# A seven-product feed-forward: two plain first tiles, no additions on POOL, two weight sums by an accumulating DMA, sums read from PSUM

## The chip, the cores and the metric

The kernel runs on one core of one Trainium2 chip. A core has five engines that run their own queues in order and wait for each other by semaphores: PE (TensorE) multiplies matrices, DVE (VectorE) and ACT (ScalarE) do arithmetic on 128 partitions and reach both SBUF and PSUM, POOL (GpSimd) does arithmetic in SBUF and issues DMAs of its own kind, SP (SyncE) issues the other DMAs. Matrix products land in PSUM, in 8 banks of 128 x 512 floats. The metric is the device time of the whole program in microseconds (us); lower is better.

## What is computed

One inference step of a small two-layer backbone of width 1024 over 640 tokens: 512 latent tokens and 128 context tokens, which are held side by side as columns 0 to 511 and 514 to 641 of a feature-major tile of 642 columns (512 and 513 are a gap of zeros). Every sub-layer is an RMSNorm, a shift and scale that come from the conditioning vector, the sub-layer itself, and a gated addition to the residual stream. The part of the reference that the change touches is the feed-forward of the second layer and the output projection ahead of it:

```python
def conv_ffn(h, w_up, conv_w, conv_b, w_down):
    a, b = jnp.split(h @ w_up, 2, axis=-1)
    a = dwconv(a, conv_w, conv_b)
    return (jax.nn.silu(a) * b) @ w_down
...
        x = x + g1 * (mix @ p['w_out'][i])
        h = rmsnorm(x, p['norm_ffn'][i]) * (1.0 + sc2) + sh2
        x = x + g2 * conv_ffn(h, p['ffn_w_up'][i], p['ffn_conv_w'][i], p['ffn_conv_b'][i], p['ffn_w_down'][i])
```

`w_up` has 2 x 2816 columns: 22 tiles of 128 columns for `a` and 22 for `b`.

## The kernel before

**Precision.** Every operand of the large products is split into a rounded part and a rest (`h` and `l`). ACT writes the rounded part (a cast), DVE subtracts it from the source for the rest, and `mm3` (lines 302 to 306) issues three matmuls for one product: high by high, high by low, low by high.

**Seven products.** In the second layer the feed-forward takes a tile `f` of `a` and the tile `f` of `b` together. The two weight tiles are a 2 x 2 block matrix (rows: the first and the last 512 features; columns: `a` and `b`), and the tokens are cut in two blocks of 320. Both factors are thus 2 x 2 blocks, and Winograd's form of Strassen's scheme makes the four blocks of the result from seven block products in place of eight, at the price of sums of blocks of both factors. `Blocks` holds the token blocks a11, a12, a21, a22 and the sums s1 to s4; `norm_blocks` fills them; `block_weights` makes the weights' sums (four additions of 128 x 512 on DVE per tile) and splits the seven weight operands; `up_unit` issues the seven products (12 matmuls of 320 columns each) into PSUM banks X, Y and V, keeps four of them in SBUF by ACT copies (`keep`: q1, u2, q5, u3), and adds: `ar` and one part of `br` on DVE, the other part of `br` on POOL from two SBUF copies (line 603). `give` then does the convolution, the SiLU and the gate, and splits the result into `g`; the rest `g.l` is a POOL subtraction (line 633).

**Order of the work.** `project_out` multiplies by an output weight matrix, 8 output tiles `d`, in two halves of the columns: `HALVES` 0 to 383 and 384 to 641. With a follower (`then`) the first four tiles run whole, and the last four run first half by first half and then second half by second half. After the first of the second halves, `norm_stats` makes the first half's norm factors (squares summed over partitions by matmuls with a column of ones, the power on POOL, a broadcast by matmuls, an ACT copy to `rb`); after the second of them `then(0, rb)` is called, which for this layer is `norm_blocks` of half 0. After the last tile come `norm_stats` and `norm_blocks` of half 1. The token blocks are cut at column 320 and the halves at 384, so half 0 fills a11 and a12 whole and 64 columns each of a21 and a22; half 1 fills their rest, and makes and splits the sums.

`ffn_blocks` runs 22 tiles in groups of 8, 7 and 7 (`FGROUPS`), each group followed by a `project_out` of the down projection. Only a11 and a12 exist early, so in the first group the first two products of tiles 0 and 1 are issued ahead (`next(u)`) before either tile goes on.

**What sets the order on an engine.** The framework queues each engine's instructions at build time: an instruction earlier in the program goes first, but one that is expected to have its inputs sooner may be put ahead of it. A tile with `bufs=n` waits for the release of the buffer n tiles back. The raw weights (`wr`) have 3 buffers. The split weights have 4 rooms (2 pools of 2); `split_w` takes a room, `split_op` half a room. While the last four tiles of `project_out` are open they hold all four rooms.

**Layer 0** has the same `project_out` with the same follower scheme, but a plain feed-forward (`ffn`): its follower `into` splits the first two weight pairs into `pre`, and `ffn` multiplies four first halves before it needs any second half.

Of the kernel before, what the change touches and what calls it, by code (L numbers as in the profile page):

```python
# [81 lines left out]
def hybrid_kernel(ctx: ExitStack, tc: tile.TileContext, A, O):  # L82
# [280 lines left out]
    def norm_stats(acc, rb, hf, last=None):  # L363

        cs = HCHUNKS[hf]
        n = len(cs)
        ps = s_ps("ss")  # L370
        for i, t in enumerate(cs):
            c = slice(COFF[t], COFF[t] + 128)
            nc.tensor.matmul(ps[:, i : i + 1], acc[:, c], ones, start=True, stop=last is None)
# [3 lines left out]
        nc.vector.tensor_scalar(out=v, in0=ps[:, :n], scalar1=1.0 / D, scalar2=EPS, op0=ALU.mult, op1=ALU.add)
        rs = tmp.tile([P, 3], F32, tag="nr", name=nm("nr"))[:, :n]
        rsqrt(rs, v, n)
        ps = s_ps("rb")  # L380
        for i in range(n):
            nc.tensor.matmul(ps[:, BLK[i]], rs[:, i : i + 1].broadcast_to([P, P]), ident, start=True, stop=True)
        if last is not None:
            return ps
        if hf == 0:
            nc.scalar.copy(rb[:, :384], ps[:, :384])
        else:
            nc.gpsimd.memset(rb[:, 512:514], 0.0)
            nc.scalar.copy(rb[:, 384:512], ps[:, :128])
            nc.scalar.copy(rb[:, PO:NT], ps[:, 128:256])  # L390
# [82 lines left out]
    class Blocks:  # L473
# [18 lines left out]
        def split(self, n, k, src, eng=None):  # L492
            if n not in self.hi:
                self.hi[n], self.lo[n] = (slot(n + t_, (P, 4, ST), F32R) for t_ in "hl")
            h_ = self.hi[n][:, k, :]
            nc.scalar.copy(h_, src)
# [5 lines left out]
    def norm_blocks(x, rb, layer, w, B, hf):  # L502

        c0, c1 = HALVES[hf]

        def norm(d):
            k, f = d % 4, d // 4
            t = tmp.tile([P, NT], F32, tag="ft" if d % 2 else "fs", name=nm("nt"))
            nc.vector.tensor_tensor(out=t[:, c0:c1], in0=x[d // 2][:, d % 2, c0:c1], in1=rb[:, c0:c1], op=ALU.mult)
            for i, parts in enumerate(SPARTS):  # L510
                to = B.raw((("a11", "a12"), ("a21", "a22"))[i][f], k)
                for a, b, o in parts:
                    a_, b_ = max(a, c0), min(b, c1)
                    if a_ < b_:
                        m = 0 if a < PO else 1
                        nc.scalar.activation(
                            to[:, o + a_ - a : o + b_ - a], t[:, a_:b_], AF.Identity,
                            scale=scl[:, layer, w, d, m : m + 1], bias=mcol(layer, 0 if w == 0 else 3, d, m),
                        )

        if hf == 0:
            for d in range(KD):
                norm(d)
                n = ("a11", "a12")[d // 4]
                B.split(n, d % 4, B.raw(n, d % 4), nc.vector if d % 2 == 0 else nc.gpsimd)
            return
        for k in range(4):
            norm(k)
            norm(k + 4)
            a11, a12, a21, a22 = (B.raw(n, k) for n in ("a11", "a12", "a21", "a22"))  # L530
            s1 = tmp.tile([P, NT], F32, tag="fs", name=nm("s1"))[:, :ST]
            nc.vector.tensor_tensor(out=s1, in0=a22, in1=a21, op=ALU.subtract)
            nc.vector.tensor_tensor(out=a11, in0=a11, in1=a21, op=ALU.subtract)
            nc.vector.scalar_tensor_tensor(out=a21, in0=a11, scalar=-1.0, in1=a22, op0=ALU.mult, op1=ALU.subtract)
            nc.vector.scalar_tensor_tensor(out=a12, in0=a21, scalar=-1.0, in1=a12, op0=ALU.mult, op1=ALU.subtract)
            for n, src in (("s2", a21), ("s1", s1), ("s3", a11), ("s4", a12), ("a22", a22)):
                B.split(n, k, src)
# [1631 lines left out]
```

## Time and profile before

| | us |
|---|---|
| median of 3 runs (1921.46 to 1929.83) | 1925.57 |
| the profiled execution | 1924.54 |
| its span, first to last instruction | 1922.7 |
| what lies around the span | 1.84 |
| PE busy (share of the span) | 1821.7 (95%) |
| DVE busy | 1311.0 (68%) |
| ACT busy | 791.1 (41%) |
| POOL busy | 424.0 (22%) |
| mean granted TensorE clock | 0.983 |

Busy time of PE is not PE at its peak, since a matmul's record overlaps the next one's. So the text below reads PE by the starts of its matmuls. A group of instructions is shown as: line, engine, operation, output<-inputs, shapes, count, then busy time and mean of one, then the idle time ahead of them and who ended it. A stage of the windows view shows for each engine the busy time and, in brackets, how many instructions it had, then the granted clock, the DMA share and GB/s.

### The profile page before, as it was taken

The numbers are of one execution on the slowest core, as the hardware profiler recorded it, in microseconds if no ns is written. First come the engines' busy times: TensorE is split into PE (matmuls) and PEld (weight loads), VectorE is DVE, ScalarE is ACT, GpSimd is POOL, SyncE is SP. The second block draws the span as 40 slices with busy tenths as digits, with TensorE's granted clock in tenths as the row PEclk, the third lists the DMA queues.
The fourth block names the chain that finished last, engine by engine and source line by source line (L and its number), as shares of the span: only waits on it lengthen the run. The fifth ranks groups of instructions, "written<-read, shape, count | busy, mean of one in ns | idle before, by whom it ended". The sixth has DMA issues, their size and how long they took to land. (4 is left out here: it accounts for less than half of the span.)

```text
span 1922.7 us, 31316 instructions
## 1 busy us (share of the span) xinstructions
PE 1821.7 (95%) x12248; PEld 1694.0 (88%) x12248; DVE 1311.0 (68%) x2624; ACT 791.1 (41%) x1544; POOL 424.0 (22%) x445
## 2 busy tenths in 40 slices
PE   5899999999889999999999999999997999999998
PEld 1578999998667999999999998978796999999998
DVE  4755666667797669757677647655648974875974
ACT  3555443343232263313312324544537651652653
POOL 2323442325554011101100103410001220220221
PEclk9899999999999999999999999999997999999999
DMA  8332112225453335434343222201211231222221
GB/s 287 123 102 75 44 46 73 71 65 188 155 189 105 143 144 187 133 129 143 115 160 127 75 90 99 92 23 50 78 45 44 88 100 55 78 83 72 88 88 56
DMA packets 66189, 197.46 MB, mean 103 GB/s; under 512 B 6872, under 2 KB 18520, under 8 KB 65914
## 3 DMA queue, kind: packets, MB, share of 16 engines
q1 hardware_dynamic: 52000, 176.71, 27.3%
q10 hardware_dynamic: 14042, 18.76, 2.8%
q8 instruction: 96, 1.57, 0.3%
q14 instruction: 51, 0.42, 0.1%
HBM read 178.91 MB, written 16.54 MB: 102 GB/s over the span
## 5 line engine op out<-in xcount | busy, mean ns | idle before, releaser
L298 ACT CAST wwh<-wr 128x1024 fp32r<-128x1024 f32 (+1 forms) x136 | 139.1, 1023 | 302.9 <-PE mm L305 277.4
L305 PE MATMUL mm<-h1l,wwh 128*128 128x384 f32 (+2 forms) x704 | 219.0, 311 | 0.9 <-DVE h1l L406 0.9
L306 PE MATMUL mm<-h1h,wwl 128*128 128x384 f32 (+2 forms) x704 | 218.9, 311 | 0.0
L304 PE MATMUL mm<-h1h,wwh 128*128 128x384 f32 (+2 forms) x704 | 218.5, 311 | 0.0
L299 DVE TENSOR_TENSOR wwl<-wr,wwh 128x1024 fp32r<-128x1024 f32 (+1 forms) x136 | 167.6, 1233 | 60.3 <-ACT wwh L298 60.1
L422 DVE SCALAR_TENSOR_TENSOR x<-mm,mod,x 128x128 f32<-128x128 f32 (+1 forms) x192 | 78.2, 436 | 168.6 <-PE mm L306 168.5
L250 DVE SCALAR_TENSOR_TENSOR mjunk<-mraw,crow 128x512 f32<-128x512 f32 x192 | 150.3, 795 | 2.7 <-ACT crow L238 1.5
L304 PE MATMUL mm<-h0h,wwh 128*128 128x384 f32 (+2 forms) x448 | 148.9, 332 | 0.5 <-DVE d L823 0.2
L305 PE MATMUL mm<-h0l,wwh 128*128 128x384 f32 (+2 forms) x448 | 140.3, 313 | 0.0
L306 PE MATMUL mm<-h0h,wwl 128*128 128x384 f32 (+2 forms) x448 | 139.4, 311 | 0.0
L699 DVE SCALAR_TENSOR_TENSOR cv<-mm,par,cv 128x382 f32<-128x382 f32 (+3 forms) x184 | 100.2, 546 | 57.2 <-ACT cv L693 56.1
L305 PEld LDWEIGHTS mm<-h1l,wwh 128*128 128x128 f32 x704 | 133.1, 189 | 1.8 <-DVE h1l L406 1.6
L306 PEld LDWEIGHTS mm<-h1h,wwl 128*128 128x128 f32 x704 | 132.9, 189 | 0.0
L304 PEld LDWEIGHTS mm<-h1h,wwh 128*128 128x128 f32 x704 | 132.6, 188 | 0.2 <-ACT h1h L405 0.2
L550 ACT CAST cwh<-wr 128x512 fp32r<-128x512 f32 x132 | 79.5, 622 | 79.8 <-PE mm L305 23.2
L551 DVE TENSOR_TENSOR cwl<-wr,cwh 128x512 fp32r<-128x512 f32 x132 | 99.4, 772 | 12.5 <-ACT cwh L550 12.4
L304 PE MATMUL od<-owh,h2h 128*128 128x256 f32 x320 | 98.4, 308 | 0.4 <-ACT h2h L405 0.4
L1112 POOL TENSOR_TENSOR am<-a,msk 128x512 fp32r<-128x512 f32 x60 | 73.0, 1225 | 91.9 <-PE Q L1141 81.3
L306 PE MATMUL od<-owh,h2l 128*128 128x256 f32 x320 | 90.5, 286 | 1.9 <-DVE h2l L406 1.1
L305 PE MATMUL od<-owl,h2h 128*128 128x256 f32 x320 | 90.7, 284 | 0.0
L693 ACT ACTIVATE cv<-mm,par 128x383 f32<-128x383 f32 x92 | 50.6, 550 | 94.5 <-PE mm L306 89.7
L304 PEld LDWEIGHTS mm<-h0h,wwh 128*128 128x128 f32 x448 | 85.4, 191 | 3.1 <-issue 1.8
(540 smaller groups left out, 5479.5 us busy)
## 6 DMA issues: line engine op xcount, KB each, us to landing
wr<-in_w_up SPq DMA_DIRECT2D x88, 512.0 KB, 3.2
wr<-in_w_mod SPq DMA_DIRECT2D x48, 512.0 KB, 4.5
mraw<-in_w_modT SPq DMA_DIRECT2D x48, 512.0 KB, 3.5
wr<-in_w_in SPq DMA_DIRECT2D x28, 512.0 KB, 3.3
wr<-in_w_dn SPq DMA_DIRECT2D x32, 448.0 KB, 3.3
wr<-in_w_out SPq DMA_DIRECT2D x16, 512.0 KB, 3.2
wr<-in_w_dn SPq DMA_DIRECT2D x16, 512.0 KB, 3.6
wr<-in_od_w_in SPq DMA_DIRECT2D x16, 512.0 KB, 4.0
```

What stands on the lines that cost most here:

```text
L250: nc.vector.scalar_tensor_tensor(out=junk, in0=raw[:, c], scalar=1.0, in1=rows[m][:, c], op0=ALU.mult, op1=ALU.mult, accum_out=part[:, d, ...
L298: nc.scalar.copy(hi[:, :K], src)
L299: nc.vector.tensor_tensor(out=lo[:, :K], in0=src, in1=hi[:, :K].bitcast(F32), op=ALU.subtract)
L304: nc.tensor.matmul(ps, l[0](k), r[0](k), start=start, stop=False, skip_group_check=more)
L305: nc.tensor.matmul(ps, l[0](k), r[1](k), start=False, stop=False, skip_group_check=more)
L306: nc.tensor.matmul(ps, l[1](k), r[0](k), start=False, stop=stop, skip_group_check=more)
L422: nc.vector.scalar_tensor_tensor(out=xt[:, a:b], in0=ps[:, a - c0 : b - c0], scalar=mcol(layer, ch, d, m), in1=xt[:, a:b], op0=ALU.mult, o ...
L550: nc.scalar.copy(hi, src)
L551: nc.vector.tensor_tensor(out=lo, in0=src, in1=hi.bitcast(F32), op=ALU.subtract)
L693: nc.scalar.activation(t[:, o0:o1], p[:, o0 - a : o1 - a], AF.Identity, scale=w[1], bias=0.0 if bias is None else bias)
L699: nc.vector.scalar_tensor_tensor(out=t[:, c0:c1], in0=p[:, c0 + s_ - a : c1 + s_ - a], scalar=w[i], in1=t[:, c0:c1], op0=ALU.mult, op1=ALU ...
L1112: eng.tensor_tensor(out=v(out), in0=v(a32), in1=msk[:, lv, :, None, :].broadcast_to([P, 2, 2, P]), op=ALU.mult)
```

## The change

- `project_out` of layer 1, `norm_stats` and `residual` take the cut of the halves as an argument. The new cut `SCUT` is 0 to 319 and 320 to 641, the cut of the token blocks, so that half 0 fills a11 and a12 and half 1 fills a21 and a22. The norm factors of a half are made for chunks of 128 or 64 tokens, with one DVE and one POOL operation per run of chunks of equal height (for `SCUT` two of each, one before). With `SCUT` the last square isn't added into `acc`, and half 1 reads its factors from PSUM, without the ACT copies.
- `then(0, rb)` is called after the last tile's second half (`soon=3`), not after the second tile's.
- The follower `to_blocks` splits the weights of tiles 0 and 1 (`up_w`) into `pre`.
- Tiles 0 and 1 of the feed-forward are plain (`plain_unit`): 8 products a tile, first both tiles' columns 0 to 319, then the rest.
- The sums of the token blocks are made behind the first halves, by `combine`, for two feature blocks at a time (128 x 640), half of them ahead of tile 0's second half and half ahead of tile 1's.
- `block_weights`: two plain loads of 256 KB put w11 and w12 into a new tile `t13`, and a DMA that POOL issues adds the whole `b` tile (w12 and w22 side by side) onto it, so that `t13` holds t1 and t3. Two additions on DVE remain. `t13` has 2 buffers.
- `up_unit`: the part of `br` that POOL added is added on DVE, straight from PSUM bank X; the copy `u3` goes. All seven products of a tile are issued in one go.
- `give`: `g.l` and, in `norm_blocks`, every rest is made on DVE, none on POOL. The scratch for POOL's DMAs grows from 1024 to 2048.

```diff
+CUT = (HALVES, HPARTS, (((0, 128), (128, 256), (256, 384)), ((384, 512), (PO, NT))))
+SCUT = (
+    ((0, 320), (320, NT)), (((0, 320, 0),), ((320, 512, 0), (PO, NT, 1))),
+    (((0, 128), (128, 256), (256, 320)), ((320, 384), (384, 512), (PO, NT))),
+)
...
-                if hf == 1 and d == first + 1:
+                if hf == 1 and d == first + soon:
                     then(0, rb)
...
     def norm_blocks(x, rb, layer, w, B, hf):
...
+        c0, c1 = SCUT[0][hf]
+        for k in range(4):
+            for f in range(2):
+                d, n = k + 4 * f, ("a11", "a12", "a21", "a22")[2 * hf + f]
+                t = tmp.tile([P, NT], F32, tag="ft" if f else "fs", name=nm("nt"))
+                r_ = rb[:, c0:c1] if hf == 0 else rb[:, : c1 - c0]
+                nc.vector.tensor_tensor(out=t[:, c0:c1], in0=x[d // 2][:, d % 2, c0:c1], in1=r_, op=ALU.mult)
+                to = B.raw(n, k)
+                for a, b, o in SPARTS[hf]:
+                    m = 0 if a < PO else 1
+                    s_, b_ = scl[:, layer, w, d, m : m + 1], mcol(layer, 0 if w == 0 else 3, d, m)
+                    if m:
+                        nc.vector.tensor_scalar(
+                            out=to[:, o : o + b - a], in0=t[:, a:b], scalar1=s_, scalar2=b_, op0=ALU.mult, op1=ALU.add
+                        )
+                    else:
+                        nc.scalar.activation(to[:, o : o + b - a], t[:, a:b], AF.Identity, scale=s_, bias=b_)
+                B.split(n, k, to)
+
+    def combine(B, k):
+
+        kk = slice(k, k + 2)
+        a11, a12, a21, a22 = (B.raws[n][:, kk, :] for n in ("a11", "a12", "a21", "a22"))
+        s1 = tmp.tile([P, NT], F32, tag="fs", name=nm("s1"))[:, : 2 * ST].rearrange("p (k t) -> p k t", k=2)
+        nc.vector.tensor_tensor(out=a11, in0=a11, in1=a21, op=ALU.subtract)
+        nc.vector.tensor_tensor(out=s1, in0=a22, in1=a21, op=ALU.subtract)
+        nc.vector.scalar_tensor_tensor(out=a21, in0=a11, scalar=-1.0, in1=a22, op0=ALU.mult, op1=ALU.subtract)
+        B.split("s2", kk, a21)
+        B.split("s1", kk, s1)
+        B.split("s3", kk, a11)
+        nc.vector.scalar_tensor_tensor(out=a12, in0=a21, scalar=-1.0, in1=a12, op0=ALU.mult, op1=ALU.subtract)
+        B.split("s4", kk, a12)
...
-    def block_weights(a, b, pool):
+    def block_weights(layer, f, pool):
...
+        t13 = pool.tile([P, 1024], F32, tag="t13", name=nm("t13"), bufs=2)
+        nc.sync.dma_start(t13[:, :512], w_a[:, :512])
+        nc.sync.dma_start(t13[:, 512:], w_b[:, :512])
+        nc.gpsimd.dma_start(t13, w_b, accum_op=ALU.add)
+        t1, t3 = (t13[:, 512 * i : 512 * i + 512].rearrange("p (k c) -> p k c", k=4) for i in range(2))
+        a = load_raw(w_a, KD)
+        w11, w21 = a[:, :4], a[:, 4:]
+        w22 = load_raw(w_b[:, 512:], 4)
         yield split_op(w11)
         yield split_op(w21)
...
+        TT(out=w11, in0=t1, in1=w22, op=ALU.add)
         yield split_op(w11)
+        yield split_op(t1)
+        yield split_op(t3)
         yield split_op(w22)
-        TT(out=w21, in0=w21, in1=t2, op=ALU.add)
+        TT(out=w21, in0=w21, in1=w11, op=ALU.add)
         yield split_op(w21)
...
+    def plain_unit(wa, wb, f, B, outs, give):
+
+        ar, br = (outs[f % 2][:, i, :] for i in range(2))
+        for hf in range(2):
+            ps = []
+            for w in (wa, wb):
+                ps.append(mm_ps("pu"))
+                for k in range(KD):
+                    n = ("a11", "a12", "a21", "a22")[2 * hf + k // 4]
+                    l, r = wl_of(w), B.of(n)
+                    mm3(ps[-1][:, :ST], l, ((lambda k: r[0](k % 4)), (lambda k: r[1](k % 4))), k, k == 0, k == KD - 1)
+            for a, b, o in SPARTS[hf]:
+                nc.scalar.copy(ar[:, a:b], ps[0][:, o : o + b - a])
+                nc.vector.tensor_copy(br[:, a:b], ps[1][:, o : o + b - a])
+            if hf == 0:
+                yield
+        give(f, ar, br, 1.0)
...
-        u3 = keep("u3", X)
         for a, b, o in SPARTS[1]:
-            nc.gpsimd.tensor_tensor(out=br[:, a:b], in0=u3[:, o : o + b - a], in1=q5[:, o : o + b - a], op=ALU.add)
+            nc.vector.tensor_tensor(out=br[:, a:b], in0=X[:, o : o + b - a], in1=q5[:, o : o + b - a], op=ALU.add)
...
-                nc.gpsimd.tensor_tensor(out=g.l(k, 0, NT), in0=s, in1=g.h(k, 0, NT).bitcast(F32), op=ALU.subtract)
+                nc.vector.tensor_tensor(out=g.l(k, 0, NT), in0=s, in1=g.h(k, 0, NT).bitcast(F32), op=ALU.subtract)
...
+                us = [plain_unit(*pre[2 * f : 2 * f + 2], f, B, outs, give) for f in range(2)]
+                for u in us:
+                    next(u)
+                for k, u in zip((0, 2), us):
+                    combine(B, k)
+                    next(u, None)
+                f1 = 2
+            for f in range(f1, f0 + n):
+                up_unit(layer, f, B, pool, outs, give)
...
+    def to_blocks(hf, rb):
+        if hf == 0:
+            norm_blocks(x, rb, 1, 1, hb, hf)
+            pre.extend((up_w(1, 0), up_w(1, NF)))
+        else:
+            pre.extend((up_w(1, 1), up_w(1, NF + 1)))
+            norm_blocks(x, rb, 1, 1, hb, hf)
+
+    project_out(x, mix, 1, 2, wout(1), KD, to_blocks, cut=SCUT, soon=3)
```

More of the change, by code (lines that the diff above doesn't have):

```diff
@@ L385, in norm_stats @@
         if hf == 0:
-            nc.scalar.copy(rb[:, :384], ps[:, :384])
+            c1 = cut[0][0][1]
+            nc.scalar.copy(rb[:, :c1], ps[:, :c1])
         else:
             nc.gpsimd.memset(rb[:, 512:514], 0.0)
-            nc.scalar.copy(rb[:, 384:512], ps[:, :128])
-            nc.scalar.copy(rb[:, PO:NT], ps[:, 128:256])
+            for a, b, _ in cut[1][1]:
+                nc.scalar.copy(rb[:, a:b], ps[:, a - c0 : b - c0])
     def norm_mod(x, rb, layer, w, act, hf, ds=range(KD)):
@@ L416, in sq_acc, with residual @@
             nc.vector.tensor_tensor(out=acc[:, c0:c1], in0=acc[:, c0:c1], in1=q[:, c0:c1], op=ALU.add)
-    def residual(x, d, ps, layer, ch, hf):
+    def residual(x, d, ps, layer, ch, hf, cut=CUT):
         xt = x[d // 2][:, d % 2, :]
-        c0 = HALVES[hf][0]
-        for a, b, m in HPARTS[hf]:
+        c0 = cut[0][hf][0]
+        for a, b, m in cut[1][hf]:
             nc.vector.scalar_tensor_tensor(
@@ L431, in load_x, with project_out @@
         return x
-    def project_out(x, act, layer, ch, wsrc, K, then=None, post=None, between=iter(()), ws=()):
+    def project_out(x, act, layer, ch, wsrc, K, then=None, post=None, between=iter(()), ws=(), cut=CUT, soon=1):
         acc = new_acc() if then else None
@@ L442, in out @@
         def out(d, w, hf):
-            ps = run(proj_half(w, act, K, HALVES[hf]))
-            residual(x, d, ps, layer, ch, hf)
+            ps = run(proj_half(w, act, K, cut[0][hf]))
+            residual(x, d, ps, layer, ch, hf, cut)
             if then:
-                q = sq_acc(acc, x[d // 2][:, d % 2, :], d == 0, *HALVES[hf], last=post and hf == 1 and d == KD - 1)
+                q = sq_acc(
+                    acc, x[d // 2][:, d % 2, :], d == 0, *cut[0][hf], last=(post or cut is SCUT) and hf == 1 and d == KD - 1
+                )
                 if post:
@@ L502, in norm_blocks @@
     def norm_blocks(x, rb, layer, w, B, hf):
[L504 to L518, printed above, removed]
-                        )
@@ L521, in norm_blocks @@
[L521 to L537, printed above, removed]
+        c0, c1 = SCUT[0][hf]
@@ L585, in keep @@
             return q
-        ws = block_weights(load_raw(A["w_up"][layer, f], KD), load_raw(A["w_up"][layer, NF + f], KD), pool)
+        ws = block_weights(layer, f, pool)
         ar, br = (outs[f % 2][:, i, :] for i in range(2))
@@ L608, in up_unit, with ffn_blocks @@
             nc.scalar.copy(ar[:, a:b], X[:, o : o + b - a])
-        give(f, ar, br)
-    def ffn_blocks(x, B, layer, then, post, gstack):
+        give(f, ar, br, -1.0)
+    def ffn_blocks(x, B, layer, then, post, gstack, pre):
         gpool = B.pool
```

77 lines of the change are left out of this document (40 added, 37 removed).

## The prediction

> **What bounds the kernel now.** First the page's busy shares, then the stages (windows), then PE's waits, then DVE's timeline around the longest wait.
>
> ```profile
> PE 1821.7 (95%) x12248; PEld 1694.0 (88%) x12248; DVE 1311.0 (68%) x2624; ACT 791.1 (41%) x1544; POOL 424.0 (22%) x445
> ```
>
> PE is the bound on the whole, so an edit counts only by the time in which PE isn't fed, or by matmuls added. To see that time I need the price of one matmul when it is fed: two starts in a stretch without waits, 36 matmuls (three products) apart.
>
> ```profile
> 1487.50 0.31 PE L304 MATMUL bx<-s3h,cwh 128*128 128x320 f32 x1
> ...
> 1492.79 0.31 PE L304 MATMUL bx<-a11h,cwh 128*128 128x320 f32 x1
> ```
>
> 5.29 us / 36 = 0.147 us a matmul, so 1.76 a product and 12.3 a tile of 84. Now the stages: the first tiles (from the last matmul of the output projection to the start of tile 2), the other tiles of the three groups, and the same place in layer 0.
>
> ```profile
> core 0: us, PE busy (x) PEld busy (x) DVE busy (x) ACT busy (x) POOL busy (x), PEclk, DMA share, GB/s
> ...
> 1443.42:1492.79 49.37, 36.70 (x179) 31.40 (x178) 41.57 (x88) 35.57 (x83) 7.48 (x9) 0.76 0.13 43
> ...
> 1492.79:1570.69 77.90, 75.18 (x507) 73.98 (x505) 70.52 (x93) 49.19 (x96) 22.00 (x19) 1.00 0.29 96
> 1628.85:1717.99 89.14, 87.42 (x591) 86.30 (x590) 76.03 (x104) 53.75 (x104) 20.47 (x20) 1.00 0.26 86
> 1769.39:1858.72 89.33, 87.32 (x591) 86.27 (x589) 76.54 (x105) 53.70 (x105) 22.49 (x24) 1.00 0.28 92
> 689.59:710.50 20.91, 18.66 (x105) 17.23 (x104) 13.44 (x26) 15.99 (x40) 7.31 (x9) 1.00 0.65 243
> ```
>
> Tiles 0 and 1 are 168 matmuls, 24.7 us of work, and take 49.4: **24.7 us lost in one place**. The other 20 tiles (6, 7, 7) have 73.9, 86.2 and 86.2 us of work and take 77.9, 89.1 and 89.3: 10.0 lost in all. The change can win at most these two sums and a little at the groups' ends.
>
> The first loss comes from a chain and from the clock:
>
> ```profile
> 1455.24 0.16 DVE L377 TENSOR_SCALAR nv<-ss 128x2 f32<-128x2 f32 x1 [3.97 <-PE ss L373]
> ...
> 1457.82 1.44 DVE L509 TENSOR_TENSOR nt<-x,rb 128x258 f32<-128x258 f32 x4 [0.62 <-ACT rb L390]
> ...
> 1460.00:1470.00 10.00, 4.98 (x12) 3.14 (x12) 9.87 (x25) 7.40 (x20) 0.00 (x0) 0.50 0.31 105
> 1470.00:1480.00 10.00, 7.96 (x23) 6.05 (x24) 10.00 (x24) 7.98 (x19) 0.00 (x0) 0.50 0.00 1
> ...
> PE bx L304 <- ACT s2h L496: 4.9, 1, 4.9
> ```
>
> The second half's factors start only 12 us after the last output matmul (1443.42 to 1455.24), because its residuals and squares stand in DVE's and ACT's queues behind the norms of the first half. Then DVE is full (9.87 and 10.00 of 10 us) with the sums s1 to s4, while PE has used up a11 and a12 (7 us of work), waits 4.9 us for s2, and then runs at a granted clock of 0.50 with 12 and 23 matmuls in 10 us. So the critical resource there is **DVE**, with nothing on PE to cover it.
>
> **The change, part by part. (1) The start.** Tiles 0 and 1 become plain: 2 x 96 = 192 matmuls, 28.2 us, 3.5 more than now. In exchange PE has 14.1 us on columns 0 to 319 before it needs the second half, and 14.1 us on the second half while the sums are made. The output projection costs the same (320 + 322 columns in place of 384 + 258), so 1443.42 stays its end. What must be ready when, with these durations:
>
> ```profile
> L509 DVE TENSOR_TENSOR nt<-x,rb 128x258 f32<-128x258 f32 x8 | 2.9, 426 | 0.6 <-ACT rb L390 0.6
> L533 DVE TENSOR_TENSOR a11r<-a11r,a21r 128x320 f32<-128x320 f32 x4 | 1.9, 488 | 0.0
> L401 DVE TENSOR_SCALAR nt<-nt,scl,mod x24: 332/343/1016, 1162.3 to 1190.3; 128x128 f32<-128x128 f32 x16, 128x384 f32<-128x384 f32 x8
> L422 DVE SCALAR_TENSOR_TENSOR x<-mm,mod,x 128x128 f32<-128x128 f32 x40 | 12.2, 345 | 26.5 <-PE mm L306 26.5
> L630 DVE SCALAR_TENSOR_TENSOR fs<-fs,ab x22: 818/829/1226, 1490.9 to 1863.9; 128x642 f32<-128x642 f32 x22
> L625 DVE SCALAR_TENSOR_TENSOR cv<-ab,par,cv 128x641 f32<-128x641 f32 x44 | 38.9, 884 | 4.2 <-ACT cv L623 3.6
> L187 POOL TENSOR_TENSOR nr<-nv,mhalf 128x3 f32<-128x3 f32 (+1 forms) x4 | 3.9, 967 | 126.1 <-DVE nv L377 126.1
> ...
> 1447.22 0.68 DVE L565 TENSOR_TENSOR wr<-wr 128x512 f32<-128x512 f32 x1
> 1447.83 0.68 DVE L568 TENSOR_TENSOR wr<-wr,t 128x512 f32<-128x512 f32 x1
> ```
>
> In a run without waits DVE's instructions start 0.08 us closer than they last (1447.22 to 1447.83: 0.61), so I take 0.08 off each. First half: eight products with the factors and eight rests, all now on DVE, 16 x 0.41 = 6.6 us; with the residuals and squares they fit between the first half's factors (some 5 us behind tile 4's second half, near 1435.5) and 1446. PE may wait 0.5 us for the last blocks of a11, and 0.7 for the small matmuls of the factors: 1.2. Second half: since the follower now comes behind the residuals, the chain residual 0.6 with its wait 0.5, square 0.4, sums 0.6, two scalings 0.3, two powers 1.9 (one more than now, +1.0), broadcast 0.7, hand-overs 0.6 puts its factors at 1449. From there DVE has: the norms, 8 x (0.41 + 0.25 + 0.41) = 8.6; two `combine` of eight operations of 640 columns, 16 x 0.75 = 12.0; four pairs of `br` copies at 0.6, 2.4; the gate and convolution of tile 0, 2 x 0.80 + 2 x 0.75 = 3.1; the rest of tile 2's first weights, 0.6. Sum 26.7, so tile 2 can start at 1475.7. PE is there at 1443.4 + 1.2 + 28.2 = 1472.8: it waits 2.9. Tile 2's third product needs s2 and three more weight operations (1.8) behind tile 1's gate (3.1): 1480.6, where PE is at 1479.2: 1.4. For what DVE still owes after that I add 0.7. **Stalls 6.2**, so 34.4 us in place of 49.4: **15.0 won**. Bounds: layer 0 shows the same scheme without sums and loses 20.9 - 96 x 0.175 = 4.1 us; with nothing but the 2 us that PE cannot avoid I get 19 won; with tile 2's weights behind everything that DVE owes (13 us of stalls) 8 won. Layer 0's stage has a granted clock of 1.00, and none of my waits is as long as the 4.9 that stood ahead of 0.50.
>
> [...]
>
> **(2) The steady tiles.** PE's remaining waits, and what stretches DVE:
>
> ```profile
> PE bv L304 <- ACT q L584: 3.8, 7, 0.8
> PE bx L304 <- ACT u L584: 2.6, 2, 1.4
> ...
> L562 DVE TENSOR_TENSOR t<-wr,wr x22: 683/693/1965, 1438.7 to 1838.2; 128x512 f32<-128x512 f32 x22
> L568 DVE TENSOR_TENSOR wr<-wr,t x22: 676/686/2073, 1447.8 to 1842.7; 128x512 f32<-128x512 f32 x22
> ...
> L551 DVE TENSOR_TENSOR cwl<-wr,cwh 128x512 fp32r<-128x512 f32 x132 | 99.4, 772 | 12.5 <-ACT cwh L550 12.4
> L603 POOL TENSOR_TENSOR ab<-u,q 128x192 f32<-128x192 f32 (+1 forms) x44 | 36.3, 845 | 173.3 <-ACT u L584 173.3
> L562 DVE TENSOR_TENSOR t<-wr,wr 128x512 f32<-128x512 f32 x22 | 24.5, 1114 | 0.4
> L568 DVE TENSOR_TENSOR wr<-wr,t 128x512 f32<-128x512 f32 x22 | 24.1, 1096 | 0.0
> ```
>
> The same addition takes 0.68 or up to 2.07 us; the long ones lie beside POOL's additions. Over 0.69 the three groups hold 9.3 + 8.9 + 11.2 = 29 us, 1.3 a tile. That delays a split on ACT, behind it the copies q5 and u2, and behind these PE. DVE's own work stays: two weight additions go (1.2), the `br` part (0.6) and `g.l` (0.75) come. ACT loses a copy (0.33). What is unknown is whether POOL's writing of DMA descriptors holds DVE up as its additions did: between nothing and the same 1.3 a tile. Bank X now waits for two DVE reads in place of one ACT copy before the seventh product may write it; the sixth product (1.76 us) covers 0.6 us of reads, but not a DVE queue that is late. I take **4.0 won** of the 10.0 (bounds: 0 and 9).
>
> [...]
>
> ```profile
> L594 DVE TENSOR_TENSOR ab<-by,q 128x320 f32<-128x320 f32 x22 | 10.7, 485 | 0.2
> ```
>
> [...]
>
> **(3) The accumulating DMA.** A tile moves 1,792 KB in place of 1,024; the DMA share of 0.3 in the stages leaves room. Its own duration X is not in the trace. Nearest rows, both for 512 KB:
>
> ```profile
> wr<-in_w_up SPq DMA_DIRECT2D x88, 512.0 KB, 3.2
> ...
> w<-in_hy_w ACTq DMA_DIRECT2D x2, 512.0 KB, 10.7
> ```
>
> A `t13` buffer is taken by the loads (3.2), by X, and until its last split, three products on (5.3); with two buffers and 12.75 us a tile (89.2 / 7) it may take 25.5, so X may reach 17. Both rows lie under that: **nothing**, hidden under the tile before.
>
> **(4) The groups' ends.** PE waits there for the last `g.l`:
>
> ```profile
> PE mm L305 <- POOL g11l L633: 0.7, 1, 0.7
> PE mm L305 <- POOL g12l L633: 0.7, 1, 0.7
> PE mm L305 <- POOL g10l L633: 0.5, 1, 0.5
> ...
> L633 POOL TENSOR_TENSOR g10l<-fs,g10h x8: 1318/1571/1807, 1493.0 to 1577.6; 128x642 fp32r<-128x642 f32 x8
> ```
>
> DVE does it in 0.83 in place of 1.57, so most of each wait goes: **1.5 won** (0 to 1.9).
>
> **Sum.** 15.0 + 4.0 + 1.5 = 20.5 off the profiled execution's 1924.54: **1904.0 us**. That execution lies 1.0 under the median 1925.57, within the runs' spread. By the bounds: 1894.6 (19 + 9 + 1.9) to 1916.5 (8 + 0 + 0).
>
> **The rivals. A, DVE takes the place of the wait.** The 26.7 us that DVE has before tile 2 leave no slack; if its queue puts the norms or tile 2's weights late (13 us of stalls), and POOL's descriptors hold it as the additions did, 8 + 0 + 1.5 is won: 1915, spread 1912 to 1921. For it: DVE at 9.87 and 10.00 of 10. Against it: 28 us of PE work now lie beside that DVE work, where 7 did.
>
> **B, slower: the accumulating DMA sets the pace.** If X passes 17, each tile lasts (3.2 + X + 5.3) / 2. The late `t13` also stands in DVE's queue ahead of sums. At X = 20 a tile takes 14.25, 20 tiles lose 30, less 15 won at the start: 1940; at X = 24 it is 1980. [...] Against: it would need twice the slowest 512 KB on the page.
>
> **C, it doesn't do what it says:** the waits in the steady tiles aren't POOL's, nothing is won there, and the start wins its 15: 1908. This lies in the forecast's range. **D, better:** the start loses only what layer 0 loses or less and the steady tiles run clean: under 1896.
>
> **How the numbers follow.** Forecast with C, 1896 to 1912: 0.62. A: 0.20. No gain at all, 1921 to 1935, where several halves fail: 0.05. B: 0.07. D: 0.06. Range 1895 to 1920: it leaves out most of D, B, and the end of A. A measurement tells about 0.5% apart, 9.6 us: faster means under 1916. Faster: 0.62 + 0.06 + half of A = 0.78; same: the rest of A and the 0.05, 0.15; slower: 0.07.
>
> **What would show it.** In the profile after: from the last output matmul to tile 2's first about 33 us with the granted clock near 1.00 and no wait over 3 us; 0.69 as the mean of the weight additions; tiles of 12.5 us; the accumulating DMA landing in 3 to 11 us. Wrong, if PE waits there for casts of s2 or for weights of tile 2 over 5 us, if DVE's means stay stretched beside POOL, or if DVE's additions wait for `t13`.

## The result, and the profile after

| | before | after |
|---|---|---|
| median, us (5 runs each) | 1925.17 (1921.46 to 1929.83) | 1906.67 (1902.05 to 1911.03) |
| ratio, 95% interval | | 0.9906 (0.9881 to 0.9931) |
| span of the profiled execution, us | 1922.7 | 1904.9 |

One execution of `start_soon1` (an experiment below) fell in a slow state, at 3528.10 us against 1898.78 to 1906.78 for its others, and is left out of its ratio.

The page of after, first its busy shares, then a row of its DMAs:

```profile
PE 1819.6 (96%) x12282; PEld 1698.4 (89%) x12282; DVE 1279.2 (67%) x2632; ACT 773.6 (41%) x1486; POOL 363.0 (19%) x396
...
t<-in_w_up POOLq DMA_DIRECT2D x20, 512.0 KB, 5.5
```

The shares hardly move. What tells is the time per stage, so I cut the part of the program that the change touches at the first matmul of each stage: from the first matmul behind the output projection to tile 2, tiles 2 to 7, a down projection, tiles 8 to 14, a down projection, tiles 15 to 21, the last down projection with the final norm. The windows of after:

```profile
core 0: us, PE busy (x) PEld busy (x) DVE busy (x) ACT busy (x) POOL busy (x), PEclk, DMA share, GB/s
1447.45:1482.61 35.16, 33.82 (x211) 33.05 (x211) 31.13 (x66) 27.57 (x56) 1.57 (x4) 0.90 0.07 21
1482.61:1561.62 79.01, 76.25 (x507) 75.18 (x506) 66.45 (x110) 47.51 (x89) 5.16 (x6) 0.98 0.60 158
1561.62:1618.89 57.27, 57.18 (x386) 56.78 (x385) 23.72 (x39) 11.47 (x16) 0.54 (x1) 1.00 0.20 64
1618.89:1705.09 86.20, 86.20 (x590) 86.20 (x589) 67.48 (x112) 50.92 (x97) 5.44 (x7) 1.00 0.60 153
1705.09:1755.23 50.14, 49.97 (x339) 49.55 (x337) 22.61 (x39) 10.52 (x15) 0.00 (x0) 1.00 0.22 70
1755.23:1841.46 86.23, 86.23 (x590) 86.23 (x589) 68.58 (x113) 51.15 (x98) 4.69 (x9) 1.00 0.50 129
1841.46:1897.74 56.28, 53.83 (x362) 52.74 (x360) 26.50 (x48) 23.92 (x51) 8.61 (x6) 0.99 0.15 52
```

And the down projections of before:

```profile
1570.69:1628.84 58.15, 57.48 (x387) 56.84 (x385) 24.01 (x40) 11.46 (x16) 1.32 (x1) 1.00 0.19 63
1717.99:1769.38 51.39, 50.41 (x339) 49.77 (x338) 23.01 (x40) 10.49 (x15) 1.56 (x1) 1.00 0.19 58
1858.72:1915.96 57.24, 54.18 (x362) 52.87 (x360) 25.39 (x47) 23.97 (x51) 10.12 (x7) 0.98 0.15 51
```

| us | to tile 2 | tiles 2-7 | 8-14 | 15-21 | three down projections | whole stretch |
|---|---|---|---|---|---|---|
| before | 49.4 | 77.9 | 89.1 | 89.3 | 166.8 | 472.5 |
| after | 35.2 | 79.0 | 86.2 | 86.2 | 163.7 | 450.3 |

The reader is to see two things. The groups of seven tiles now run at PE's own speed: 86.20 us, all of it busy, for the 86.2 us of work that the prediction counted. And the start is better but not clean: 7.0 us over its 28.2 us of work up to tile 2, and in tiles 2 to 7 another 5.1 over 73.9.

**The loss up to tile 2.** ACT's timeline in after (start, duration, instruction, and in brackets the idle time ahead of it and who ended it):

```profile
1437.85 0.43 ACT L409 COPY rb<-rb 128x320 f32<-128x320 f32 x1 [1.81 <-PE rb L402]
1440.27 1.05 ACT L303 CAST wwh<-wr 128x1024 fp32r<-128x1024 f32 x1 [2.00 <-PE mm L310]
...
1447.41 1.05 ACT L303 CAST wwh<-wr 128x1024 fp32r<-128x1024 f32 x1 [2.15 <-PE mm L310]
...
1448.73 0.64 ACT L548 ACTIVATE a11r<-nt,mod,scl 128x320 f32<-128x320 f32 x1
```

The first half's factors are there at 1438.3, but its first activation runs at 1448.73. Ahead of it in ACT's queue stand casts of the plain weights, each of which waits some 2 us until PE frees a room (so does the last tile's square, for which PE waits below). PE's side of it, in the windows:

```profile
1447.45:1450.39 2.94, 1.78 (x14) 1.68 (x13) 2.21 (x4) 2.94 (x6) 0.00 (x0) 0.86 0.20 71
1450.39:1456.81 6.42, 6.24 (x23) 5.64 (x23) 4.74 (x14) 5.86 (x13) 1.57 (x4) 0.53 0.26 82
```

PE has nothing but the 12 one-column matmuls of the norm for 2.9 us, and then runs 22 matmuls (3.2 us of work) in 6.4 us at a granted clock of 0.53. Its longest wait in the first of these windows, from its timeline:

```profile
1448.88 0.28 PE L380 MATMUL ss<-ones,sq 128*64 128x1 f32 x2 [1.16 <-ACT sq L436]
```

**The loss in tile 2.** PE's timeline there:

```profile
1484.82 0.31 PE L310 MATMUL bv<-s1l,cwh 128*128 128x320 f32 x1
1487.63 0.64 PE L311 MATMUL by<-a12h,cwl 128*128 128x320 f32 x1 [2.50 <-DVE cwl L577]
1488.06 0.47 PE L309 MATMUL by<-a12h,cwh 128*128 128x320 f32 x1
1488.33 0.47 PE L310 MATMUL by<-a12l,cwh 128*128 128x320 f32 x1
```

PE enters tile 2 without a wait, then stands 2.5 us for the rest of its second weight, and the matmuls behind it start 0.27 us apart in place of 0.147. With that 4.1 us are lost in tile 2 (2.7 and 1.4), and 1.0 in the other five tiles of the group.

**18.5 and 22.2.** The stretch fell by 22.2 us and the medians by 18.5. The profiled run of after reached the stretch 4.0 us later than that of before (1447.45 against 1443.42). 0.6 of it lie in the output projection, which the change cuts anew; the other 3.4 lie in code that is the same in both, and are all there by 570 us (0.3 at 550 us). The same window of before and of after:

```profile
560.00:570.00 10.00, 10.00 (x75) 8.34 (x74) 8.67 (x16) 3.62 (x7) 7.77 (x9) 1.00 0.49 148
```

```profile
560.00:570.00 10.00, 10.00 (x53) 8.49 (x54) 6.85 (x12) 2.78 (x5) 5.18 (x5) 0.72 0.27 77
```

The granted clock was 0.72 there in place of 1.00, with 53 matmuls in place of 75. The last experiment asks whether the change does this.

### The profile page after: what moved, and what is told of

Read it like the earlier page. It is cut to its first block, busy times and chain, and to the rows that moved or that the text cites. A ratio compares the mean times of both kernels' runs of the same rounds, so it can differ in the third digit from the quotient of the medians.

```text
span 1904.9 us, 31390 instructions
## 1 busy us (share of the span) xinstructions
PE 1819.6 (96%) x12282; PEld 1698.4 (89%) x12282; DVE 1279.2 (67%) x2632; ACT 773.6 (41%) x1486; POOL 363.0 (19%) x396
## 5 line engine op out<-in xcount | busy, mean ns | idle before, releaser
L303 ACT CAST wwh<-wr 128x1024 fp32r<-128x1024 f32 (+1 forms) x140 | 143.6, 1025 | 313.5 <-PE mm L310 285.9
L304 DVE TENSOR_TENSOR wwl<-wr,wwh 128x1024 fp32r<-128x1024 f32 (+1 forms) x140 | 171.9, 1228 | 54.7 <-ACT wwh L303 54.3
L445 DVE SCALAR_TENSOR_TENSOR x<-mm,mod,x 128x128 f32<-128x128 f32 (+3 forms) x192 | 78.2, 436 | 166.3 <-PE mm L311 166.3
L576 ACT CAST cwh<-wr 128x512 fp32r<-128x512 f32 x100 | 60.0, 622 | 79.0 <-PE mm L310 22.5
L588 POOL DMA_DIRECT2D t<-in_w_up x20 | 17.3, 867 | 378.2 <-DMA t<-in_w_up 152.6
```

Source lines behind the costliest of these rows:

```text
L303: nc.scalar.copy(hi[:, :K], src)
L304: nc.vector.tensor_tensor(out=lo[:, :K], in0=src, in1=hi[:, :K].bitcast(F32), op=ALU.subtract)
L445: nc.vector.scalar_tensor_tensor(out=xt[:, a:b], in0=ps[:, a - c0 : b - c0], scalar=mcol(layer, ch, d, m), in1=xt[:, a:b], op0=ALU.mult, o ...
L576: nc.scalar.copy(hi, src)
```

## The experiments

All times below are read as above. Ratios are to the kernel before, timed on the same chip.

### The order of the start

`start_soon1` calls the first half's norms after the second output tile:

```diff
-    project_out(x, mix, 1, 2, wout(1), KD, to_blocks, cut=SCUT, soon=3)
+    project_out(x, mix, 1, 2, wout(1), KD, to_blocks, cut=SCUT, soon=1)
```

> The kernel after with one number changed: the first half's norms (and the first two plain weights) are asked for after the second output tile's second half (soon=1) in place of after the fourth. Theory Q (queue order): in the kernel after, the 6.9 us lost between the last output matmul and tile 2 come from ACT's queue, where the casts of the plain weights, each waiting some 2 us for a room, stand ahead of the first half's activations, so that PE finds no a11 and its clock falls. Then here a11 is ready when the output projection ends, the stretch from the last output matmul to tile 2's first product falls from 35.2 to about 29.5 us (28.2 of work), and the whole by about 6 us, to 1901. Rival D (DVE is full): the second half's factors and DVE's 27 us of work before tile 2 set that moment whatever the order; then what is won ahead of tile 2 is lost again inside tile 2 (4.1 us there become about 9), and the whole stays within 2 us of 1906.7.

Its windows up to tile 2, for tiles 2 to 7, and for eight us within tile 2:

```profile
1450.83:1482.44 31.61, 30.67 (x213) 30.07 (x211) 27.66 (x59) 21.09 (x42) 1.98 (x4) 1.00 0.07 26
1482.44:1562.13 79.69, 76.42 (x506) 75.42 (x505) 67.70 (x110) 48.53 (x92) 5.16 (x6) 0.98 0.57 156
...
1484.00:1488.00 4.00, 3.41 (x22) 2.94 (x21) 4.00 (x7) 3.76 (x8) 0.00 (x0) 1.00 0.00 0
1488.00:1492.00 4.00, 2.42 (x10) 2.16 (x11) 4.00 (x8) 1.56 (x2) 0.00 (x0) 0.74 0.02 4
```

The dip of the clock is gone (1.00 in place of 0.90) and 3.6 of the 7.0 us with it, but 0.7 come back in tiles 2 to 7: the stretch is 447.4 us, ratio 0.9872 (0.9846 to 0.9899). Both theories hold for a part. The queue order cost 3.6 us up to tile 2, not the 5.7 that theory Q asked for: 3.4 us stay. They are the second half's norm in PE's queue: the 12 one-column matmuls take 1.3 us, and the six broadcast matmuls behind the power on POOL 2.0, from 1455.91 to 1457.91:

```profile
1456.10 0.43 PE L402 MATMUL rb<-ident,nr 64*128 64x64 f32 x2
1457.44 0.71 PE L402 MATMUL rb<-ident,nr 128*128 128x128 f32 x4 [0.91 <-POOL ab L662]
```

Inside tile 2, DVE is busy for 4.00 of 4 us twice while PE has 3.41 and 2.42. So `start_light` takes work off DVE:

```diff
+    project_out(..., soon=1)
-        nc.vector.tensor_tensor(out=lo[:, :K], ...)
+        (eng or nc.vector).tensor_tensor(out=lo[:, :K], ...)
+            pre.extend((up_w(1, 0, nc.gpsimd), up_w(1, NF, nc.gpsimd)))
+            pre.extend((up_w(1, 1, nc.gpsimd), up_w(1, NF + 1, nc.gpsimd)))
-                nc.vector.tensor_copy(br[:, a:b], ps[1][:, o : o + b - a])
+                nc.scalar.copy(br[:, a:b], ps[1][:, o : o + b - a])
```

> The kernel after with soon=1 and two things taken off DVE at the start: the four rests of the plain tiles' weights go to POOL (4.9 us of DVE), the br copies of tiles 0 and 1 to ACT (8 instructions, 2.4 us of DVE). Theory D (DVE is full): with soon=1 the norms came in time (31.8 us from the last output matmul to tile 2 in place of 35.4, the clock never halved there), and the 4.4 us that PE still lost inside tile 2 and the 1.3 in tile 3 are DVE's queue, which is full from 1458 to 1493. With 7.3 us less on DVE they fall under 1.5 us together: the stretch from the last output matmul to the last matmul's end goes from 447.5 to about 443, the whole to about 1900. Rival C (contention): POOL's long subtractions stretch DVE's two-input work beside them as they did in the steady tiles, or ACT becomes the late one; then the stretch stays at 446 to 449 us and the whole within 3 us of 1903.6.

Measured: 32.84 us to tile 2, 76.12 for tiles 2 to 7, the stretch 445.2 us, ratio 0.9874 (0.9852 to 0.9897). Tiles 2 to 7 win 3.6, so DVE's work was most of the loss there; the start gives back 1.2. DVE's and then POOL's timeline of this kernel:

```profile
1438.28 2.41 DVE L439 TENSOR_TENSOR acc<-acc,sq 128x322 f32<-128x322 f32 x1 [0.51 <-ACT sq L436]
```

```profile
1437.95 2.38 POOL L304 TENSOR_TENSOR wwl<-wr,wwh 128x1024 fp32r<-128x1024 f32 x1 [38.58 <-ACT wwh L303]
1440.30 1.49 POOL L394 TENSOR_TENSOR nr<-nv,mhalf 128x2 f32<-128x2 f32 x2
```

An addition that takes 0.49 us without POOL's subtraction beside it (`start_soon1`) lasts 2.41 and ends 0.36 us after POOL's subtraction does; the power of the norm stands behind that subtraction in POOL's queue too. That is the contention that rival C named: DVE's work lasting longer beside POOL's. `start_light2` therefore leaves the first pair on DVE:

```diff
-            pre.extend((up_w(1, 0, nc.gpsimd), up_w(1, NF, nc.gpsimd)))
+            pre.extend((up_w(1, 0), up_w(1, NF)))
```

> As start_light, but only the second pair of the plain tiles' rests goes to POOL, behind the power of the second half's norm; the first pair stays on DVE. In start_light POOL's subtraction of 128 x 1024 (2.4 us) stood ahead of the power and stretched the DVE instruction beside it: two additions of squares to 2.41 us from 0.49, and a scaling to 3.26 from 0.34; that cost the stretch up to tile 2 1.2 us (33.0 against 31.8 with soon=1 alone), while inside tiles 2 to 7 2.9 us were won. Theory C (contention): without the first pair on POOL the stretch up to tile 2 falls back to 31.8 us or a little more, the tiles 2 to 7 stay at 76 us, and from the last output matmul to the last matmul's end it takes 443.5 to 444.5 us in place of 445.3; the whole near 1900. Rival D (DVE is full): the 2.4 us of DVE work that come back push tile 2's weights late again, and the sum stays at 445 to 447 us.

```profile
1445.94:1478.41 32.47, 32.21 (x213) 31.61 (x212) 28.07 (x55) 23.26 (x49) 5.97 (x6) 0.95 0.07 25
1478.41:1553.26 74.85, 74.49 (x506) 73.91 (x505) 64.84 (x106) 47.82 (x91) 5.14 (x6) 1.00 0.63 166
```

Tiles 2 to 7 now lose 1.0 us, the stretch is 443.1 us, and the median 1899.95 against 1928.24 of before in the same runs: 0.9856 (0.9839 to 0.9872). Its stretch is the shortest of all, 7.2 us under that of after; its ratio lies clear of after's, but not of those of `start_soon1` and `start_light`.

Up to tile 2 only 0.4 of the 1.2 us came back. Contention is no longer the reason: the second half's power starts 4.7 us into the stretch, as in `start_soon1`, in place of 6.1 in `start_light`. The clock fell instead:

```profile
1451.87 1.23 PE L402 MATMUL rb<-ident,nr 128*128 128x128 f32 x4 [0.23 <-POOL nr L394]
...
1452.75:1455.27 2.52, 2.52 (x11) 2.52 (x11) 2.13 (x3) 0.55 (x1) 2.52 (x2) 0.51 0.02 7
```

The nine matmuls of 320 columns that start in this window take 2.5 us in place of 1.3, behind the same small matmuls as in `start_soon1` and with no wait over 0.23 us ahead of them. So in this run an early a11 alone didn't keep the clock up.

### Which part made the steady tiles clean

Each kernel is after with parts put back as before: `br`'s part through an ACT copy and POOL (B), `g.l` on POOL (G), four weight additions on DVE from whole tiles in place of the accumulating DMA (S). Where B stands without S, the copy uses the buffer of q1; where it stands with S, a buffer of its own.

```diff
B  +        u3 = keep("q1", X)
   -            nc.vector.tensor_tensor(out=br[:, a:b], in0=X[:, o : o + b - a], ...)
   +            nc.gpsimd.tensor_tensor(out=br[:, a:b], in0=u3[:, o : o + b - a], ...)
G  -                nc.vector.tensor_tensor(out=g.l(k, 0, NT), ...)
   +                nc.gpsimd.tensor_tensor(out=g.l(k, 0, NT), ...)
S  -        nc.gpsimd.dma_start(t13, w_b, accum_op=ALU.add)
   +        TT(out=w11, in0=w11, in1=w12, op=ALU.add)
   +        TT(out=t2, in0=w11, in1=w22, op=ALU.add)
   +        TT(out=w12, in0=w12, in1=w22, op=ALU.add)
   +        TT(out=w21, in0=w21, in1=t2, op=ALU.add)
```

> The kernel after with one addition put back: the part of br is copied out of PSUM by ACT and added on POOL (44 POOL instructions), as before. Theory S (stretch): it was POOL's additions that stretched DVE's weight additions from 0.69 up to 2.07 us and with them cost PE in the steady tiles. Then the mean of the two weight additions left rises from 0.69 to about 1.1, and of the 9.0 us that the 20 tiles gained, 5 to 9 come back: groups of seven tiles at 88 to 89 us in place of 86.2, the whole near 1913. Rival A (accumulating DMA): the tiles gained because two additions left DVE; then the groups stay within 0.5 us of 86.2 and the whole within 2 us of 1906.7.

> The kernel after without the accumulating DMA: all four additions of a tile's weights on DVE again, from the two whole weight tiles; br and g.l stay on DVE. Theory S (stretch): nothing on POOL stretches DVE, so the additions take 0.69 each, DVE has 1.2 us more a tile (some 78% busy in place of 68%), and PE loses nothing by it: groups of seven at 86.2 to 86.7 us, the whole within 2 us of 1906.7. Rival A (accumulating DMA): the tiles' gain came from taking two additions off DVE; then 5 to 9 us come back, groups at 88 to 89 us, the whole near 1913.

> The kernel after with the rest g.l subtracted on POOL again (22 instructions). Theory E (ends): of the 3.1 us that the three down projections gained, all comes from g.l, which took 1.57 us on POOL and takes about 0.75 on DVE; then the three stretches from the first down matmul to the next group's first product grow by about 1 us each (57.3, 50.1 and 56.3 in the kernel after), the steady tiles lose up to 1 us in all by stretched DVE work, and the whole rises by 3 to 4 us to about 1910. Rival: the ends gained through the last tile's earlier br and ar; then the stretches stay within 0.3 us each and the whole within 1 us.

> The kernel after with its three steady parts put back: all four weight additions on DVE from the two whole tiles (no accumulating DMA), the part of br added on POOL from a third ACT copy, and g.l on POOL. What is left of the change is the start. Theory I (interplay): one part alone cost the seven-tile groups nothing (86.4, 86.6 and 86.4 us against 86.2) because DVE keeps slack; only POOL's work and the long queue of additions together make DVE late enough for PE. Then here the groups are back at 88.5 to 89.3 us and the whole near 1914 to 1916. Rival P (place in the queue): the tiles were faster for another reason, that a tile's seven products are issued in one go and the first two tiles no longer run seven-product; then the groups stay at 86.2 to 86.8 us, only the ends (2.6 us) come back, and the whole stays under 1911.

> The kernel after with two parts put back: g.l on POOL, and all four weight additions on DVE; br stays on DVE, from PSUM. Theory I1: g.l on POOL is what stretches an addition to 1.7 to 2.0 us (it stood beside 8 of the long ones before, and beside all 6 long ones where g.l alone was put back), and with four additions in DVE's queue PE feels it: groups of seven at 88 to 89 us, some 5 to 8 us of the tiles' gain back, the whole near 1916. Rival I2: br's way over an ACT copy and POOL is needed too (its copy u3 takes ACT time ahead of q5 and u2, which PE waited for); then the groups stay at 86.3 to 86.9 and only the ends' 2.6 us and tile 2's 1 us come back: near 1911.

> The kernel after with br's part on POOL (from an ACT copy) and all four weight additions on DVE, g.l left on DVE. Theory G: g.l on POOL is what starts the loss, since it is long (1.57 us) and stands beside an addition in every tile; with br alone on POOL no addition was stretched. Then the groups of seven stay at 86.2 to 86.8 us, the whole within 3 us of 1906.7. Rival: POOL's work of either kind is enough once DVE has four additions a tile; then the groups lose 2 us or more each, the whole near 1913.

> The kernel after with both additions on POOL again (br's part from an ACT copy, and g.l), but with the accumulating DMA, so two weight additions on DVE. Theory I: without the four additions in DVE's queue PE doesn't feel the stretch; groups of seven at 86.2 to 86.9 us, the ends' 2.6 us and about 1 us in tile 2 come back, the whole near 1911. Rival: the stretch alone costs; then the groups are at 88 us or more, as with all three parts back (89.5 and 88.1), and the whole near 1916.

| us | put back | tiles 2-7 | 8-14 | 15-21 | three down projections | stretch | ratio (95%) |
|---|---|---|---|---|---|---|---|
| after | none | 79.0 | 86.2 | 86.2 | 163.7 | 450.3 | 0.9906 (0.9881 to 0.9931) |
| steady_br_pool | B | 79.3 | 86.4 | 86.2 | 163.9 | 450.1 | 0.9898 (0.9878 to 0.9917) |
| steady_sums_dve | S | 79.7 | 86.6 | 86.2 | 163.8 | 451.4 | 0.9888 (0.9869 to 0.9907) |
| ends_gl_pool | G | 80.3 | 86.4 | 86.4 | 166.3 | 454.6 | 0.9920 (0.9902 to 0.9939) |
| steady_br_sums | B, S | 79.6 | 86.5 | 86.2 | 163.9 | 450.5 | 0.9886 (0.9866 to 0.9907) |
| steady_gl_br | G, B | 81.4 | 86.6 | 86.2 | 166.0 | 454.5 | 0.9896 (0.9876 to 0.9916) |
| steady_gl_sums | G, S | 83.0 | 91.8 | 90.9 | 165.8 | 465.8 | 0.9983 (0.9967 to 1.0000) |
| start_only | G, B, S | 81.8 | 89.5 | 88.1 | 166.5 | 461.1 | 0.9955 (0.9940 to 0.9971) |

Each stage is read from one profile, and two profiles of before differ by 2.3 us in the stretch (below), so a difference of 1 us in it says little. The ratios of (G, S) and (G, B, S) lie clear of that of after; the other five overlap it.

No part alone explains the steady tiles: one part put back costs a group of seven 0.4 us at most. So the stretch theory of `steady_br_pool` falls, for B alone lengthened no addition (0.69 us), and its rival A falls for S. The pairs say which belong together. Without `g.l` on POOL (B, S) and without the four additions (G, B) the groups of seven stay clean, though G and B together cost tiles 2 to 7 2.4 us; G and S together cost 5 us a group, more than all three. The lengthening of DVE's additions itself needs G alone: `ends_gl_pool`, from its groups of instructions, against 0.69 for both in after:

```profile
L601 DVE TENSOR_TENSOR wr<-wr 128x512 f32<-128x512 f32 x19 | 20.2, 1061 | 0.3
L596 DVE TENSOR_TENSOR wr<-t,wr 128x512 f32<-128x512 f32 x18 | 12.4, 689 | 2.0 <-DMA wr<-in_w_up 1.8
```

Seven us more for DVE (19 x 0.375), of which PE notices 0.4 in the two groups of seven and 1.2 in tiles 2 to 7. How it gets to PE when DVE has four additions is in `steady_gl_sums`: the waits of PE, then POOL, DVE and PE in one tile.

```profile
PE bx L309 <- DVE ab L645: 6.1, 8, 1.0
```

```profile
1661.47 1.55 POOL L675 TENSOR_TENSOR g11l<-fs,g11h 128x642 fp32r<-128x642 f32 x1 [14.57 <-ACT g11h L674]
```

```profile
1661.75 1.82 DVE L597 TENSOR_TENSOR wr<-wr,t 128x512 f32<-128x512 f32 x1
1663.48 0.68 DVE L577 TENSOR_TENSOR cwl<-wr,cwh 128x512 fp32r<-128x512 f32 x1
1664.09 0.54 DVE L645 TENSOR_TENSOR ab<-bx,q 128x192 f32<-128x192 f32 x2
```

```profile
1663.59 0.31 PE L311 MATMUL bv<-s4h,cwl 128*128 128x320 f32 x1
1664.69 0.41 PE L309 MATMUL bx<-a22h,cwh 128*128 128x320 f32 x1 [0.79 <-DVE ab L645]
```

The fourth addition is caught beside `g.l`, the read of bank X stands behind it, and the seventh product waits for X: 6.1 us in eight waits, the largest of PE's waits in these groups (the next, 2.3, is for the copy q). This is the late DVE queue that the prediction named for the sums read from PSUM. With `br` on POOL too an ACT copy frees X, and the loss is smaller; with `g.l` on DVE the additions' means stay at 0.69, or 0.78 at most (B, S).

### One buffer for the accumulated sums

`t13` with `bufs=1` in place of 2.

> The kernel after with one buffer for the tile that the accumulating DMA writes, in place of two. The formula of the prediction, (3.2 + X + 5.3) / buffers a tile, with X = 5.5 us as the kernel after shows it, gives 14.0 us a tile in place of 12.3: groups of seven near 96 us, 17 tiles with a predecessor lose 1.7 each, 29 us, the whole near 1935. Rival: the splits run up to seven operands ahead of PE, so that the buffer comes free earlier than the formula has it; then the groups stay under 90 us and the whole under 1920.

```profile
1481.54:1582.01 100.47, 82.86 (x506) 81.18 (x505) 66.61 (x110) 47.78 (x89) 5.13 (x6) 0.92 0.49 124
1639.29:1738.44 99.15, 91.28 (x591) 89.39 (x589) 67.28 (x112) 51.63 (x97) 5.11 (x6) 0.97 0.51 133
1788.59:1894.84 106.25, 92.30 (x590) 90.45 (x589) 67.90 (x113) 52.23 (x98) 5.52 (x10) 0.95 0.45 115
```

1960.66 us, ratio 1.0177 (1.0141 to 1.0214). The middle group's 14.2 us a tile (99.15 / 7) is the formula's 14.0; the others take 16.7 and 15.2, at granted clocks of 0.92 and 0.95. The rival falls. The formula's 1935 was too low by what these two groups took beyond 14.0 a tile, 16.5 and 8.3 us; that the clock did it is likely by these figures, but not shown apart.

### The kernel before once more

> The kernel before, unchanged, profiled once more. The changed stretch (from the first matmul behind the output projection to the last matmul's end) took 472.5 us before and 450.3 after, 22.2 us less, while the medians differ by 18.5. Theory V (varying stage): the 3.7 us lie ahead of the stretch, in code that is the same in both, where the profiled run of after was 3.4 us later from 560 to 628 us on; a second profile of before then reaches the stretch anywhere from 1442 to 1451 us, as eleven other kernels with the same code did, and the stretch itself takes 472 to 473 us again. Rival F (fixed shift): the change itself makes the earlier code some 4 us slower; then it reaches the stretch at 1443 to 1444 us again. Rival L: the stretch of before varies by some us from one run to the next, and this one takes 468 to 470 us.

Its window at the place where after had lost time:

```profile
560.00:570.00 10.00, 10.00 (x52) 8.40 (x51) 6.39 (x12) 2.34 (x4) 4.74 (x5) 0.70 0.22 62
```

The clock is down here as it was in after. It reaches the stretch at 1447.22 us, 3.8 later than the first profile of before, so the 3.4 us in the common code are no work of the change, and the fixed shift falls. (Over all profiles here the stretch is reached between 1442.1 and 1451.4 us.) The stretch took 470.3 us, 2.3 less than in the first profile (1.4 of it in tiles 15 to 21), so that varies too. The change is thus worth 20 to 22 us of the stretch, by one profile or the other, and 18.5 by the medians.

## Why the prediction was right

1904.0 was forecast, and 1906.67 came. Each part won where it was forecast to win, but the sum came so close by luck: the start was put 4.9 us too high, the tiles and the ends 6.6 us too low, and the profiled run of after reached the stretch 4.0 us late:

| us won | forecast | measured in the stages |
|---|---|---|
| start | 15.0 | 10.1 |
| steady tiles | 4.0 | 9.0 |
| groups' ends | 1.5 | 3.1 |
| accumulating DMA | 0 | 0 |
| sum | 20.5 | 22.2 |

(Start: 35.16 + 4.1 in tile 2 against 49.37, with the 4.1 counted here as the forecast counted it. Tiles: 10.0 lost before, 1.0 left.)

- **The start, "stalls 6.2": mis-sized, 11.0 measured.** The step that failed is "with the residuals and squares they fit between the first half's factors (...) and 1446". It counted DVE's work and left out ACT's queue, in which the casts of the plain weights stood ahead of the first activation; `start_soon1` puts 3.6 us on that order. The other 3.4 are the second half's small matmuls and the wait for its power, which the prediction put at 0.7. "None of my waits is as long as the 4.9 that stood ahead of 0.50" failed as well: the clock was 0.53 behind a wait of 1.16 us. The trace of before had shown that a shorter wait can stand ahead of it:

```profile
1449.68 0.57 PE L305 MATMUL by<-a12l,cwh 128*128 128x320 f32 x1 [1.78 <-POOL a12l L497]
1450.05 0.47 PE L306 MATMUL by<-a12h,cwl 128*128 128x320 f32 x1
```

  Behind 1.78 us the matmuls start 0.27 us apart, from 1450.05 to 1452.98, at a granted clock of 0.50. The wait of 2.9 at tile 2's start didn't come; it came inside tile 2, where DVE's queue had put the weights late, as rival A had it, at 4.1 us in place of 13. `start_only`, which keeps only this part of the change, takes 35.16 + 81.79 us to the end of tile 7 against 127.27 before: 10.3. (Both sums hold the steady loss in tiles 2 to 7.)
- **The steady tiles, "4.0 (0 to 9)": the direction right, the size at the upper bound.** The 4.0 left room for POOL's issuing of DMAs to hold DVE up. In after it didn't: the 20 additions of line 596 took 0.68 to 0.69 us, one of them beside an issue of 0.85 us, DVE and then POOL:

```profile
1506.81 0.69 DVE L596 TENSOR_TENSOR wr<-t,wr 128x512 f32<-128x512 f32 x1
```

```profile
1506.55 0.85 POOL L588 DMA_DIRECT2D t<-in_w_up  x1 [6.51 <-DVE fs L676]
```

  The reason given, POOL's additions beside DVE's, was right in kind. The runs narrow it: it is `g.l` that matters, and in the groups of seven only with four additions in DVE's queue. Rival C, that nothing would be won there, is out: `start_only` against after is 2.8 + 3.3 + 1.9 = 8.0 us.
- **The ends, "1.5": mis-sized, 3.1.** The forecast read the waits (0.7 + 0.7 + 0.5). They begin at the end of a matmul's record, which overlaps the next one. By starts, in before:

```profile
1724.65 0.33 PE L304 MATMUL mm<-g11h,wwh 128*128 128x384 f32 x1
1725.72 0.44 PE L305 MATMUL mm<-g11l,wwh 128*128 128x384 f32 x1 [0.73 <-POOL g11l L633]
```

  1.07 us between two starts that lie 0.17 apart when fed: 0.90 lost where the row says 0.73. Putting `g.l` back costs the ends 2.6 us, so it is most of the 3.1.
- **The accumulating DMA, "nothing": right.** X is 5.5 us, within the 3.2 to 10.7 of the nearest rows and far under 17, and the groups run without a gap. Rival B's formula is borne out by the middle group of `t13_one`. Of the signs that the prediction named, the additions' mean (0.69), the tiles and the DMA came as said; up to tile 2 the 35.2 us for some 33 and the clock of 0.90 did not.

## What to carry to other kernels

When a step is moved, walk every in-order queue that its instructions enter, the lightly used one too: here ACT's casts, each waiting for a room, cost 3.6 us that no sum of DVE's work could show. Two removals that each are worth next to nothing in a stage can be worth much together, so undo them in pairs before crediting one. Measure PE's losses from start to start against the fed spacing, not by the idle time that a wait's row gives.

## What the runs showed of the hardware

- **The clock fell without a long wait, but not every time.** In after the granted clock was 0.53 for 6.4 us behind 2.94 us with only 12 one-column matmuls and a longest wait of 1.16 us. In `start_light2` it was 0.51 for 2.5 us behind the same small matmuls and a wait of 0.23 us; in `start_soon1` and `start_light`, with waits of 0.91 and 1.6 us at the same place, it stayed at 1.00. So in these runs the length of the wait alone doesn't tell whether the clock falls, and no run isolates what does.
- **A lengthened DVE instruction ended just behind POOL's.** The two additions ended 0.36 us (squares, `start_light`) and 0.55 us (weights, `steady_gl_sums`: 1661.75 + 1.82 against 1661.47 + 1.55) after POOL's, less than their own durations without it, 0.49 and 0.69. Whether they waited for POOL's end or ran slower, no run isolates. Not all of DVE's work beside POOL's was lengthened: in `start_light` two multiplications with one of their inputs in PSUM took 0.89 us together beside POOL's subtraction, as they did without it in `start_soon1` (0.89). A scaling with one data input, right behind them, took 3.26 us in place of 0.34 and ended 0.16 us behind POOL's second subtraction:

```profile
1459.98 3.26 DVE L544 TENSOR_SCALAR a21r<-nt,scl,mod 128x128 f32<-128x128 f32 x1
```

```profile
1458.35 4.73 POOL L304 TENSOR_TENSOR wwl<-wr,wwh 128x1024 fp32r<-128x1024 f32 x2
```

- **POOL's issuing of a DMA didn't lengthen an addition.** In after the addition that started 0.26 us into an issue of 0.85 us took 0.69 us; the mean of its line is 0.69.
- **An input in PSUM cost no time here.** In before a DVE operation of 128x320 took 485 ns with one input from PSUM (line 594) and 488 with both from SBUF (line 533); in after the two additions of that size with an input from PSUM took 487 and 490 (lines 641 and 651).
